# Issue order of the feed-forward stages of a two-layer encoder trunk: chunks earlier, sums in steps, tables in pieces, splits one output late

## The chip, the core and the metric

The kernel runs on one core of one Trainium2 chip. The metric is device time in microseconds (us) of one execution, the median of several runs. The core's engines work in parallel, each through its own instructions in a fixed order, and wait for each other by semaphores: TensorE (PE in the profile, with its weight loads as PEld) multiplies matrices, VectorE (DVE), ScalarE (ACT) and GpSimd (POOL) work elementwise, SyncE (SP) issues transfers. A result of PE lies in a bank of the accumulator memory until another engine has read it.

## The reference

A trunk of two layers on one sequence of 512 tokens of width 1024, all in float32. A layer is a half-step SwiGLU feed-forward stage, a mixer (latent attention, a bidirectional mLSTM and a Fourier part beside each other), a second feed-forward stage and a gated embedding:

```python
def swiglu(x, w_gate, w_up, w_down):
    return (jax.nn.silu(x @ w_gate) * (x @ w_up)) @ w_down
...
h = x
for i in range(DEPTH):                                    # DEPTH = 2
    h = h + 0.5 * swiglu(rmsnorm(h, ffn1_norm[i]), ffn1_w_gate[i], ffn1_w_up[i], ffn1_w_down[i])
    u = rmsnorm(h, mix_norm[i]) @ w_in[i]
    ...
    h = h + y @ w_out[i]
    h = h + 0.5 * swiglu(rmsnorm(h, ffn2_norm[i]), ffn2_w_gate[i], ffn2_w_up[i], ffn2_w_down[i])
    e = rmsnorm(p[i] @ ple_w_proj[i], ple_post_norm[i])
    gate = jax.nn.sigmoid(rmsnorm(h, ple_gate_norm[i]) @ ple_w_gate[i])
    h = h + gate * e
return rmsnorm(h, final_norm)
```

The inner width of a feed-forward stage is 2816, which is 22 features of 128. The attention turns parts of its queries and keys by rotary tables, cosine and sine of position times frequency.

## The kernel before, in words

**Precision by halves.** Every operand of a product is split into a high half, rounded to the matmul's type by a cast on ACT (line 134, or 353 and 415 where the split is written out), and a low half, the rest, by a subtraction on DVE (line 131, `lo_of`). A product is three matmuls: high by high, high by low, low by high (lines 161 to 163). So every weight costs an ACT cast and a DVE subtraction before PE can use it: a chunk is 128 x 1024 numbers (512 KB) that come by one transfer on SP's queue into `wraw` (two buffers) and are split into `whi` and `wlo` (three each).

**A feed-forward stage** (`ffn`, line 305) runs four times, with the mixer (`mix`) or the embedding gate (`ple`) behind it. Activations lie transposed, feature by token, in 8 rows of blocks `h[:, m]`. The first `PLAIN` = 4 features are computed plainly: a block of 24 matmuls for gate and one for up, then `gated` (DVE, ACT's silu, DVE, split). The other 18 features go by Strassen's scheme in Winograd's form with 7 products instead of 8: `p1` to `p7`, each 12 matmuls of 256 columns (line 451). On the weight side it takes the four sums S1 to S4 of quarters of the chunks: some are made by an adding transfer on POOL's queue (`acc`, line 427), two by DVE (`sums`, lines 436 and 438), and all are split by `parts` (lines 415 and 131). On the activation side it takes four sums T1 to T4, the same for all 18 features, which `combined` makes once per stage (lines 375 to 381: two scaled copies on ACT, two subtractions on POOL, two steps on DVE, a split), for four pairs of rows.

**One unit** u is a period of seven slots, in the order p6(u), p1(u+1), p7(u), p5(u+1), p4(u), p2(u+1), p3(u). p1, p6, p7 and p4 of one feature add up in one accumulator bank, and between them the bank is copied as it stands: `g1` behind p1 (line 478), `g2` behind p6 (516), `c22` behind p7 (526, and 527 on DVE). The next product into that bank waits for the copy. The rest of a unit is elementwise: lines 505 and 506 (DVE, POOL) behind p2, 536 and a split behind p4, 547 and 548 behind p3, the silus at 550 (at 594 for the first unit) and at 461, and 462 on POOL.

**Down parts.** After each group of units (`GROUPS`), a down part multiplies the group's features into all eight outputs, one block of three matmuls per feature and output; `flush` (lines 559 and 560) adds an output to `h`. In the last down part of a stage, `flush` also calls the next stage's `chunk` for the row: the high half `xh` on ACT (287), the low half `xl` on DVE (289), and a square on ACT with its addition on DVE (192, 193) for the next norm. The square root of that norm is taken by a chain of DVE steps (`wide`, lines 218 to 229) in the plain part of the next feed-forward stage, or by `tok` in the other stages.

**What sets the order.** The stage is a list written out by hand. `item(us, run, tasks)` gives a PE step a price by which a clock advances (5.6 for a plain block, 1.434 for a product, 0.7 per feature of a down output) and its preparing tasks with a lead each. All tasks are sorted by the clock of their item minus their lead, and a task is issued ahead of the first item whose clock has come to that. `tc.manual_schedule()` keeps this order on every engine. In the mixer that holds for PE alone, and elsewhere the scheduler chooses. Leads before: a chunk's transfer 12 and its split 7; transfers of quarters 17 or 24; sums and `parts` 7.

Of the kernel before, what the change touches and what calls it, by code (L numbers as in the profile page):

```python
# [10 lines left out]
F32 = mybir.dt.float32  # L11
# [20 lines left out]
LEAD = 5  # L32
H = T // 2
PLAIN = 4
GROUPS = (5, 5, 4, 4, 4)
NA = max(GROUPS) + 1
QD = 6
NB = HALF + 2
# [55 lines left out]
def trunk(ctx: ExitStack, tc, xT, pT, pos, W, gains, cst, dftc, out):  # L94
# [85 lines left out]
    class Norm:  # L180


        def __init__(self, n):
            self.n, self.acc = n, None

        def add(self, x):
            if self.acc is None:
                self.acc = sp.tile([P, T], F32, tag="sqacc", name="sqacc")
                S.activation(self.acc, x, AF.Square)
            else:  # L190
                sq = sp.tile([P, T], F32, tag="sq", name="sq", bufs=1)
                S.activation(sq, x, AF.Square)
                V.tensor_tensor(self.acc, self.acc, sq, op=ALU.add)

        def tok(self, by=None):

# [45 lines left out]
    sinT = cp.tile([P, T], F32, name="sinT")  # L242

    def rope_tables():
        def tile(tag, dt=F32, bufs=None):
            return sp.tile([P, T], dt, tag=tag, name="rope", bufs=bufs)

        pi = tile("sq", I32, 1)
        nc.scalar.dma_start(pi, pos)
        r = tile("rbc", bufs=3)  # L250
        V.tensor_copy(r, pi)
        V.tensor_scalar(r, r, cs[:, C_INV:C_INV + 1], None, op0=ALU.mult)
        k = tile("rbc", bufs=3)
        V.tensor_scalar(k, r, 1.0 / TWO_PI, None, op0=ALU.mult)
        big = 1.5 * 2.0 ** 23
        V.tensor_scalar(k, k, big, None, op0=ALU.add)
        V.tensor_scalar(k, k, -big, None, op0=ALU.add)
        k1 = tile("sqacc")
        big1 = 1.5 * 2.0 ** 34
        V.tensor_scalar(k1, k, big1, None, op0=ALU.add)  # L260
        V.tensor_scalar(k1, k1, -big1, None, op0=ALU.add)
        k0 = tile("sqacc")
        V.tensor_tensor(k0, k, k1, op=ALU.subtract)
        for m, cc in ((k1, _c1), (k0, _c1), (k1, _c2), (k0, _c2), (k, _c3)):
            V.scalar_tensor_tensor(r, m, -cc, r, op0=ALU.mult, op1=ALU.add)
        V.tensor_scalar(r, r, math.pi, -math.pi, op0=ALU.min, op1=ALU.max)
        sn = tile("sq", bufs=1)
        S.activation(sn, r, AF.Sin)
        S.activation(r, r, AF.Sin, scale=0.5)
        V.tensor_scalar(sinT, sn, cs[:, C_SGN:C_SGN + 1], None, op0=ALU.mult)  # L270
        V.tensor_tensor(r, r, r, op=ALU.mult)
        V.tensor_scalar(cosT, r, -2.0, 1.0, op0=ALU.mult, op1=ALU.add)


    h = hp.tile([P, NK, T], F32, name="h")

    class Stage:
# [5 lines left out]
            self.hi, self.lo = [None] * NK, [None] * NK  # L283

        def chunk(self, m, norm=True):
            xh = xp.tile([P, T], F32R, tag="xh", name="xh", bufs=NK)
            S.activation(xh, h[:, m], AF.Copy, scale=self.g(m))  # L287
            xl = xp.tile([P, T], F32R, tag="xl", name="xl", bufs=NK)
            V.scalar_tensor_tensor(xl, h[:, m], self.g(m), xh.bitcast(F32), op0=ALU.mult, op1=ALU.subtract)  # L289
            self.hi[m], self.lo[m] = xh, xl  # L290
            if norm:
                self.norm.add(h[:, m])

        def tok(self):
            self.rt = self.norm.tok()
# [9 lines left out]
    def ffn(l, cgu, cd, st, nxt, first=False):  # L305
# [5 lines left out]
        with tc.tile_pool(name="ap", bufs=1) as ap, tc.manual_schedule():  # L311
# [23 lines left out]
                return acts[f]  # L335


            def chunk_tasks(w, c, halves=False):

                if (l, c) in ahead:  # L340
                    w["hl"] = ahead.pop((l, c))
                    return []

                def dma():
                    w["raw"] = wp.tile([P, CHUNK], F32, tag="wraw", name="wraw", bufs=2)
                    nc.sync.dma_start(w["raw"], W[l, c])

                def prep():
                    hi = wp.tile([P, CHUNK], F32R, tag="whi", name="whi")
                    lo = wp.tile([P, CHUNK], F32R, tag="wlo", name="wlo")  # L350
                    for i in range(1 + halves):
                        b = slice(i * CHUNK // (1 + halves), (i + 1) * CHUNK // (1 + halves))
                        S.copy(hi[:, b], w["raw"][:, b])  # L353
                    lo_of(lo, w["raw"], hi)
                    w["hl"] = hi, lo

                return [(12.0, dma), (7.0, prep)]


            todo = []  # L360
            ready = 3 if first else 0
            Th, Tl = [], []

            def gated(f, pg, pu):
                t = qa()
# [5 lines left out]
            def combined(i):  # L371

                xg = tile("pw", 6, [2, T])
                for j in range(2):
                    S.activation(xg[:, j], h[:, i + 4 * j], AF.Copy, scale=st.g(i + 4 * j))
                t = tile("pw", 6, [4, H])
                (b11, b12), (b21, b22) = ((xg[:, j, 0:H], xg[:, j, H:T]) for j in range(2))
                G.tensor_tensor(t[:, 0], b11, b12, op=ALU.subtract)
                G.tensor_tensor(t[:, 1], b22, b12, op=ALU.subtract)
                V.scalar_tensor_tensor(t[:, 2], t[:, 0], -1.0, b22, op0=ALU.mult, op1=ALU.subtract)  # L380
                V.scalar_tensor_tensor(t[:, 3], t[:, 2], -1.0, b21, op0=ALU.mult, op1=ALU.subtract)
                hi, lo = tile("th", 4, [4, H], F32R), tile("tl", 4, [4, H], F32R)
                split(hi, lo, t)
                Th.append(hi)
                Tl.append(lo)

            def plain(f, i, w):
                def run():
                    if i == 0:
                        todo.append((f, bank("ps"), bank("pm")))  # L390
                    blocks(todo[-1][1 + i], *w["hl"], st)
                    n = 2 * f + i
                    if n == ready:
                        st.rb = st.norm.wide(qd)
                    if n > ready + 1 and i:
                        for x in todo:
                            gated(*x)
                        todo.clear()
                    if n > 2 * PLAIN - 5:
                        combined(n - 2 * PLAIN + 4)  # L400

                return run

# [65 lines left out]
            def p1(u, after=None):  # L469
                U[u] = {"gate": {}}  # L470

                def run():
                    d = U[u]
                    d["B"] = bank("ps")[:, 0:H]
                    hi, lo = d["gate"]["hl"]
                    product(u, "B", hi[:, 0:T], lo[:, 0:T], "B11", True)
                    d["g1"] = small("g1")
                    S.copy(d["g1"], d["B"])
                    if after is not None:
                        finish(after)  # L480

                return run, chunk_tasks(U[u]["gate"], cgu + 2 * u, True)

            def p5(u, after=None):
                def run():
# [53 lines left out]

                return run, load(u, "A22", 1) + [(7.0, lambda: parts(u, "A22"))]  # L540

            def p3(u, nxt_u):
                def run():
                    d = U[u]
                    p = d["w", "S4"]
                    product(u, "E", p[:, 0], p[:, 1], "B22", False)
                    V.tensor_tensor(d["g2"], d["g2"], d["E"], op=ALU.add)
                    G.tensor_tensor(d["g2"], d["g2"], st.rb[:, h2], op=ALU.mult)  # L548
                    if nxt_u is not None:
                        S.activation(U[nxt_u]["g1"], U[nxt_u]["g1"], AF.Silu)  # L550

                return run, [(7.0, lambda: parts(u, "S4"))]

# [3 lines left out]
            def flush(m, last):  # L557
# [1 line left out]
                V.tensor_tensor(y, pys.pop(m), st.rb, op=ALU.mult)  # L559
                V.scalar_tensor_tensor(h[:, m], y, 0.5, h[:, m], op0=ALU.mult, op1=ALU.add)  # L560
                if last:
                    nxt.chunk(m)

            def down(f0, nf, pieces, last):

                ws = {}
                for m, a, b in pieces:
                    tasks, new = [], []
                    for j in range((m * nf + a) // 8, (m * nf + b - 1) // 8 + 1):
                        if j not in ws:  # L570
                            ws[j] = {}
                            tasks += chunk_tasks(ws[j], cd + f0 + j)

                    def run(m=m, a=a, b=b):
                        if a == 0:
# [15 lines left out]
            put(SL, p1(PLAIN))  # L591
            put(SL, p5(PLAIN))
            put(SL, p2(PLAIN))
            item(0.0, lambda: S.activation(U[PLAIN]["g1"], U[PLAIN]["g1"], AF.Silu))
            g, f0 = 0, 0
            for u in range(PLAIN, NF - 1):
                prev = u - 1 if u > PLAIN else None
# [3 lines left out]
                put(SL, p5(u + 1, prev))  # L601
                put(SL, p4(u))
                put(SL, p2(u + 1))
                put(SL, p3(u, u + 1))
                if u == f0 + GROUPS[g]:
                    for x in down(f0, GROUPS[g], [(m, 0, GROUPS[g]) for m in range(NK)], False):
                        item(*x)
                    if first and g == 0:
                        item(0.0, late_constants)
                        item(0.0, rope_tables)  # L610
                    f0 += GROUPS[g]
                    g += 1
            u, n = NF - 1, GROUPS[g]
            order = [(0, 0, 2), (1, 0, 2), (2, 0, 3), (3, 0, 3), (0, 2, 4), (1, 2, 4), (2, 3, 4), (3, 3, 4)]
            ds = list(down(f0, n, order + [(m, 0, n) for m in range(4, NK)], True))
            put(SL, p6(u))
            item(*ds[0])
            item(0.0, lambda: finish(u - 1))
            put(SL, p7(u))
            item(*ds[1])  # L620
            item(0.0, lambda: finish2(u - 1))
            put(SL, p4(u))
            put(SL, p3(u, None))
            item(0.0, lambda: (finish(u), finish2(u)))
            for x in ds[2:]:
                item(*x)
# [881 lines left out]
```

## Time and profile before

| | |
|---|---|
| median of 3 runs | 2188.37 us (2185.84 to 2188.86) |
| the profiled execution | 2190.03 us, its span 2188.3 us |
| PE | busy 2035.9 us, 93% |
| DVE | busy 1565.4 us, 72% |
| ACT | busy 1015.5 us, 46% |
| POOL | busy 361.9 us, 17% |
| granted TensorE clock, mean | 0.966 |
| transfers | 244.23 MB, 240.06 MB of it read from memory, 111 GB/s over the span |

A row of a wait names the engine and line that waits, what released it, the total, how often, and the longest. A row of a timeline has the start, the duration, engine, line and operation, then output and inputs with their shapes, and in brackets the idle time before it and its releaser. A granted clock of 1.00 is full speed. The four feed-forward stages lie at about 6 to 409, 656 to 1027, 1108 to 1475 and 1725 to 2097 us.

### The profile page before, as it was taken

The page shows a single profiled execution, that of the slowest core. Times are in us where ns is not written, and L with a number is a line of the kernel's source. Part 1 is how long each engine was busy: PE and PEld are TensorE (multiplying, and loading weights), DVE is VectorE, ACT ScalarE, POOL GpSimd, SP SyncE. Part 2 cuts the span into 40 slices and gives each one's busy share as a digit, 9 for nine tenths or more (in the row PEclk, how much of TensorE's full clock was granted, in tenths as well). Part 3 has the DMA queues.
Part 4 walks back from the last instruction along what each step waited for, and adds up shares of the span by engine and source line. Part 5 has one row for each costly group of instructions (what it writes and reads, how often), then busy time and mean ns, then how long its engine had stood idle before and what let it go on. Part 6 is the DMA issues. An engine that isn't in the chain of part 4 may idle for free.

```text
span 2188.3 us, 31811 instructions
## 1 busy us (share of the span) xinstructions
PE 2035.9 (93%) x12216; PEld 1791.8 (82%) x12216; DVE 1565.4 (72%) x2607; ACT 1015.5 (46%) x1938; POOL 361.9 (17%) x415
## 2 busy tenths in 40 slices
PE   7789999899999899999998999998999989999987
PEld 5679999788777798987777989987877779899867
DVE  5677777677856677777766777776786666777777
ACT  4424444456633443444544434444575343444453
POOL 0213222000001232221002222310000022222200
PEclk9899999999999999999899999998999999999989
DMA  3345454221123445553224645522210235545421
GB/s 131 96 127 160 126 157 140 73 84 55 55 68 101 130 131 159 149 147 99 68 92 120 160 136 148 161 86 82 74 57 26 95 101 159 154 132 140 139 96 49
DMA packets 96664, 244.23 MB, mean 112 GB/s; under 512 B 10592, under 2 KB 14064, under 8 KB 96512
## 3 DMA queue, kind: packets, MB, share of 16 engines
q1 hardware_dynamic: 73488, 200.98, 27.3%
q0 software_dynamic: 20784, 37.84, 10.6%
q10 hardware_dynamic: 2240, 3.38, 0.5%
q8 instruction: 96, 1.57, 0.3%
q14 instruction: 56, 0.46, 0.1%
HBM read 240.06 MB, written 2.10 MB: 111 GB/s over the span
## 4 chain that ended last, share of the span: by engine, by line
PE 62%; DVE 17%; ACT 10%; issue 6%; POOL 3%; DMA 1%; ACTq 0%; DVEq 0%; POOLq 0%; SPq 0%
PE ps L451 12%; PE ps L163 8%; PE ps L162 8%; PE ps L161 8%; PE pm L161 7%; PE pm L163 7%; PE pm L162 7%; DVE wlo L131 4%; ACT pw L415 3%; ACT whi L353 2%; DVE pw L131 2%; PE pm L451 2%; DVE qa L436 2%; POOL g L548 1%; DVE g L505 1%
## 5 line engine op out<-in xcount | busy, mean ns | idle before, releaser
L451 PE MATMUL ps<-th,pw 128*128 128x256 f32 x2304 | 450.9, 288 | 48.2 <-ACT g L516 25.4
L451 PEld LDWEIGHTS ps<-th,pw 128*128 128x128 f32 x2304 | 374.9, 194 | 59.4 <-ACT g L516 33.6
L131 DVE TENSOR_TENSOR wlo<-wraw,whi 128x1024 fp32r<-128x1024 f32 (+3 forms) x275 | 324.5, 1181 | 79.2 <-ACT whi L134 38.4
L451 PE MATMUL ps<-tl,pw 128*128 128x256 f32 x1152 | 329.4, 286 | 0.0
L353 ACT CAST whi<-wraw 128x512 fp32r<-128x512 f32 (+1 forms) x261 | 203.4, 810 | 213.4 <-DMA wraw<-in_W 109.3
L451 PEld LDWEIGHTS ps<-tl,pw 128*128 128x128 f32 x1152 | 224.1, 195 | 0.9
L131 DVE TENSOR_TENSOR pw<-qa,pw 128x512 fp32r<-128x512 f32 x144 | 111.8, 776 | 86.8 <-ACT pw L415 85.0
L131 DVE TENSOR_TENSOR pw<-qd,pw 128x512 fp32r<-128x512 f32 x216 | 148.1, 687 | 10.9 <-ACT pw L415 5.9
L427 POOL DMA_DIRECT2D qd<-in_W x144 | 125.6, 912 | 176.6 <-DMA qd<-in_W 175.6
L161 PE MATMUL pm<-ah,whi 128*128 128x512 f32 x384 | 152.2, 396 | 0.0
L163 PE MATMUL pm<-ah,wlo 128*128 128x512 f32 x384 | 151.6, 395 | 0.0
L162 PE MATMUL pm<-al,whi 128*128 128x512 f32 x384 | 151.2, 394 | 0.0
L506 POOL TENSOR_TENSOR g<-g,rbc 128x256 f32<-128x256 f32 x72 | 72.5, 1007 | 387.4 <-DVE g L505 387.4
L134 ACT CAST whi<-wraw 128x1024 fp32r<-128x1024 f32 (+6 forms) x86 | 80.8, 943 | 116.9 <-PE ps L162 51.4
L161 PE MATMUL ps<-xh,whi 128*128 128x512 f32 x288 | 119.8, 416 | 15.7 <-ACT xh L287 12.5
L163 PE MATMUL ps<-xh,wlo 128*128 128x512 f32 x288 | 118.2, 410 | 10.8 <-DVE wlo L131 10.8
L161 PE MATMUL ps<-ah,whi 128*128 128x512 f32 x320 | 126.6, 396 | 0.0
L163 PE MATMUL ps<-ah,wlo 128*128 128x512 f32 x320 | 126.1, 394 | 0.0
L162 PE MATMUL ps<-al,whi 128*128 128x512 f32 x320 | 126.0, 394 | 0.0
L415 ACT CAST pw<-qd 128x512 fp32r<-128x512 f32 x216 | 124.0, 613 | 0.0
L162 PE MATMUL ps<-xl,whi 128*128 128x512 f32 x288 | 118.0, 410 | 1.2 <-DVE xl L289 1.1
L134 ACT CAST ah<-g 128x256 fp32r<-128x256 f32 x144 | 58.4, 406 | 124.8 <-DVE g L536 116.6
(390 smaller groups left out, 5214.0 us busy)
## 6 DMA issues: line engine op xcount, KB each, us to landing
wraw<-in_W SPq DMA_DIRECT2D x245, 512.0 KB, 3.6
qd<-in_W SPq DMA_DIRECT2D x216, 256.0 KB, 4.2
qd<-in_W POOLq DMA_DIRECT2D x144, 256.0 KB, 5.0
gr<-in_W SPq DMA_DIRECT2D x8, 512.0 KB, 3.9
wraw<-in_W SPq DMA_DIRECT2D x8, 320.0 KB, 2.8
wraw<-in_dftc SPq DMA_DIRECT2D x4, 516.0 KB, 3.4
h<-in_xT ACTq DMA_DIRECT2D x8, 256.0 KB, 4.2
wraw<-in_W SPq DMA_DIRECT2D x4, 408.0 KB, 3.0
```

What stands on the lines that cost most here:

```text
L131: V.tensor_tensor(lo, x, hi.bitcast(F32), op=ALU.subtract)
L134: S.copy(hi, x)
L161: mm(o, wh, xh, start=first, stop=False)
L162: mm(o, wh, xl, start=False, stop=False)
L163: mm(o, wl, xh, start=False, stop=last)
L353: S.copy(hi[:, b], w["raw"][:, b])
L415: S.copy(p[:, 0], U[u][src])
L427: nc.gpsimd.dma_start(U[u][name], up[:, T:2 * T] if add == "A22" else gate[:, 0:T], accum_op=ALU.add)
L436: V.tensor_tensor(d["S2"], raw[:, 0:T], d["S1"], op=ALU.add)
L451: mm(U[u][o], x[:, b], y, start=first and i + j == 0, stop=i == 3 and j == 2, skip_group_check=not first)
L505: V.tensor_tensor(d["g1"], d["g1"], d["A"], op=ALU.add)
L506: G.tensor_tensor(d["g1"], d["g1"], st.rb[:, h1], op=ALU.mult)
```

## The change

- Leads: a plain chunk's transfer 18 and split 12; a gate chunk's 15 and 9; a down chunk's 14 and 8.
- `combined` becomes a generator in two steps, the first (ACT and POOL) behind one plain block, the second (DVE and the split) behind the next, from the block at which the norm is made on (the fourth in the trunk's first stage, else the second).
- The rotary tables, which only the first feed-forward stage makes, are issued in three pieces behind the outputs 0, 4 and 6 of the first down part, not in one piece behind it.
- The silu of `g1` moves from behind p3 (and, for the first unit, from ahead of p6) to behind the copy of `g1` in the next unit's p1.
- In the last down part, the low half and the addition of the square of an output are issued behind the next output's elementwise steps; the high half and the square stay.
- Groups of (5, 4, 4, 4, 5) features, and a new order of the pieces of the last down part.

```diff
-GROUPS = (5, 5, 4, 4, 4)
+GROUPS = (5, 4, 4, 4, 5)
...
-        def add(self, x):
+        def square(self, x):
...
                 sq = sp.tile([P, T], F32, tag="sq", name="sq", bufs=1)
                 S.activation(sq, x, AF.Square)
+                self.sqs.append(sq)
+
+        def sum(self):
+            sq = self.sqs.pop(0)
+            if sq is not None:
                 V.tensor_tensor(self.acc, self.acc, sq, op=ALU.add)
...
         V.tensor_scalar(r, r, math.pi, -math.pi, op0=ALU.min, op1=ALU.max)
+        yield
         sn = tile("sq", bufs=1)
         S.activation(sn, r, AF.Sin)
         S.activation(r, r, AF.Sin, scale=0.5)
+        yield
...
+        def high(self, m, norm=True):
             xh = xp.tile([P, T], F32R, tag="xh", name="xh", bufs=NK)
             S.activation(xh, h[:, m], AF.Copy, scale=self.g(m))
+            self.hi[m] = xh
+            if norm:
+                self.norm.square(h[:, m])
+
+        def low(self, m, norm=True):
             xl = xp.tile([P, T], F32R, tag="xl", name="xl", bufs=NK)
+            V.scalar_tensor_tensor(xl, h[:, m], self.g(m), self.hi[m].bitcast(F32), op0=ALU.mult, op1=ALU.subtract)
...
+                self.norm.sum()
...
-            def chunk_tasks(w, c, halves=False):
+            def chunk_tasks(w, c, halves=False, lead=12.0):
...
-                return [(12.0, dma), (7.0, prep)]
+                return [(lead + 6.0, dma), (lead, prep)]
...
                 G.tensor_tensor(t[:, 1], b22, b12, op=ALU.subtract)
+                yield
                 V.scalar_tensor_tensor(t[:, 2], t[:, 0], -1.0, b22, op0=ALU.mult, op1=ALU.subtract)
...
                     if n == ready:
                         st.rb = st.norm.wide(qd)
+                    for x in making:
+                        next(x)
+                    making.clear()
+                    i0 = n - (3 if first else 1)
+                    if 0 <= i0 < 4:
+                        making.append(combined(i0))
+                        next(making[0])
                     if n > ready + 1 and i:
                         for x in todo:
                             gated(*x)
                         todo.clear()
-                    if n > 2 * PLAIN - 5:
-                        combined(n - 2 * PLAIN + 4)
...
                     S.copy(d["g1"], d["B"])
+                    if u > PLAIN:
+                        S.activation(U[u - 1]["g1"], U[u - 1]["g1"], AF.Silu)
                     if after is not None:
                         finish(after)
 
-                return run, chunk_tasks(U[u]["gate"], cgu + 2 * u, True)
+                return run, chunk_tasks(U[u]["gate"], cgu + 2 * u, True, 9.0)
...
                     G.tensor_tensor(d["g2"], d["g2"], st.rb[:, h2], op=ALU.mult)
-                    if nxt_u is not None:
-                        S.activation(U[nxt_u]["g1"], U[nxt_u]["g1"], AF.Silu)
...
                 if last:
-                    nxt.chunk(m)
+                    nxt.high(m)
+                    if m:
+                        nxt.low(m - 1)
+                    if m == NK - 1:
+                        nxt.low(m)
...
-                            tasks += chunk_tasks(ws[j], cd + f0 + j)
+                            tasks += chunk_tasks(ws[j], cd + f0 + j, lead=8.0)
...
-            item(0.0, lambda: S.activation(U[PLAIN]["g1"], U[PLAIN]["g1"], AF.Silu))
...
                 if u == f0 + GROUPS[g]:
-                    for x in down(f0, GROUPS[g], [(m, 0, GROUPS[g]) for m in range(NK)], False):
+                    rope = rope_tables() if first and g == 0 else None
+                    for m, x in enumerate(down(f0, GROUPS[g], [(m, 0, GROUPS[g]) for m in range(NK)], False)):
                         item(*x)
-                    if first and g == 0:
-                        item(0.0, late_constants)
-                        item(0.0, rope_tables)
+                        if rope and m in (0, 4, 6):
+                            if m == 0:
+                                item(0.0, late_constants)
+                            item(0.0, lambda rope=rope: next(rope))
...
-            order = [(0, 0, 2), (1, 0, 2), (2, 0, 3), (3, 0, 3), (0, 2, 4), (1, 2, 4), (2, 3, 4), (3, 3, 4)]
+            order = [(0, 0, 2), (1, 0, 2), (0, 2, n - 1), (1, 2, n - 1), (2, 0, n - 1),
+                     (0, n - 1, n), (1, n - 1, n), (2, n - 1, n), (3, 0, n)]
...
-            item(0.0, lambda: finish(u - 1))
+            item(0.0, lambda: (S.activation(U[u]["g1"], U[u]["g1"], AF.Silu), finish(u - 1)))
```

More of the change, by code (lines that the diff above doesn't have):

```diff
@@ L183, in __init__ @@
         def __init__(self, n):
-            self.n, self.acc = n, None
-        def add(self, x):
+            self.n, self.acc, self.sqs = n, None, []
+        def square(self, x):
             if self.acc is None:
@@ L189, in add @@
                 S.activation(self.acc, x, AF.Square)
+                self.sqs.append(None)
             else:
@@ L192, in add @@
                 S.activation(sq, x, AF.Square)
+                self.sqs.append(sq)
+        def sum(self):
+            sq = self.sqs.pop(0)
+            if sq is not None:
                 V.tensor_tensor(self.acc, self.acc, sq, op=ALU.add)
+        def add(self, x):
+            self.square(x)
+            self.sum()
         def tok(self, by=None):
@@ L285, in chunk @@
         def chunk(self, m, norm=True):
+            self.high(m, norm)
+            self.low(m, norm)
+        def high(self, m, norm=True):
             xh = xp.tile([P, T], F32R, tag="xh", name="xh", bufs=NK)
             S.activation(xh, h[:, m], AF.Copy, scale=self.g(m))
+            self.hi[m] = xh
+            if norm:
+                self.norm.square(h[:, m])
+        def low(self, m, norm=True):
             xl = xp.tile([P, T], F32R, tag="xl", name="xl", bufs=NK)
-            V.scalar_tensor_tensor(xl, h[:, m], self.g(m), xh.bitcast(F32), op0=ALU.mult, op1=ALU.subtract)
-            self.hi[m], self.lo[m] = xh, xl
+            V.scalar_tensor_tensor(xl, h[:, m], self.g(m), self.hi[m].bitcast(F32), op0=ALU.mult, op1=ALU.subtract)
+            self.lo[m] = xl
             if norm:
-                self.norm.add(h[:, m])
+                self.norm.sum()
         def tok(self):
@@ L355, in prep @@
                     w["hl"] = hi, lo
-                return [(12.0, dma), (7.0, prep)]
+                return [(lead + 6.0, dma), (lead, prep)]
             todo = []
             ready = 3 if first else 0
-            Th, Tl = [], []
+            Th, Tl, making = [], [], []
             def gated(f, pg, pu):
@@ L379, in combined @@
                 G.tensor_tensor(t[:, 1], b22, b12, op=ALU.subtract)
+                yield
                 V.scalar_tensor_tensor(t[:, 2], t[:, 0], -1.0, b22, op0=ALU.mult, op1=ALU.subtract)
@@ L385, in combined @@
                 Tl.append(lo)
+                yield
             def plain(f, i, w):
@@ L540, in p4, with p3 @@
                 return run, load(u, "A22", 1) + [(7.0, lambda: parts(u, "A22"))]
-            def p3(u, nxt_u):
+            def p3(u):
                 def run():
@@ L603, in ffn @@
                 put(SL, p2(u + 1))
-                put(SL, p3(u, u + 1))
+                put(SL, p3(u))
                 if u == f0 + GROUPS[g]:
-                    for x in down(f0, GROUPS[g], [(m, 0, GROUPS[g]) for m in range(NK)], False):
+                    rope = rope_tables() if first and g == 0 else None
+                    for m, x in enumerate(down(f0, GROUPS[g], [(m, 0, GROUPS[g]) for m in range(NK)], False)):
                         item(*x)
-                    if first and g == 0:
-                        item(0.0, late_constants)
-                        item(0.0, rope_tables)
+                        if rope and m in (0, 4, 6):
+                            if m == 0:
+                                item(0.0, late_constants)
+                            item(0.0, lambda rope=rope: next(rope))
                     f0 += GROUPS[g]
@@ L622, in ffn @@
             put(SL, p4(u))
-            put(SL, p3(u, None))
+            put(SL, p3(u))
             item(0.0, lambda: (finish(u), finish2(u)))
```

## The prediction

> **What bounds the kernel now.** I read the page's busy times and its chain first, then the engine waits of the whole span, then a table of stages.
>
> ```profile
> span 2188.3 us, 31811 instructions
> PE 2035.9 (93%) x12216; PEld 1791.8 (82%) x12216; DVE 1565.4 (72%) x2607; ACT 1015.5 (46%) x1938; POOL 361.9 (17%) x415
> PE 62%; DVE 17%; ACT 10%; issue 6%; POOL 3%; DMA 1%; ACTq 0%; DVEq 0%; POOLq 0%; SPq 0%
> ```
>
> PE is busy for 93%, but the chain that ends last is PE for only 62%: for the rest the end hangs on DVE and ACT. The change touches no matmul, so all it can do is shorten or lengthen PE's waits and the half-clock stretches behind them. The stages (columns: window, its length, busy time with instructions of PE, PEld, DVE, ACT and POOL, granted clock, DMA share, GB/s):
>
> ```profile
> 656.00:743.40 87.40, 76.13 (x401) 64.97 (x400) 56.45 (x78) 38.45 (x62) 14.96 (x17) 0.92 0.34 97
> 743.40:771.30 27.90, 27.90 (x123) 22.57 (x122) 16.75 (x23) 6.67 (x10) 4.92 (x6) 1.00 0.57 152
> 771.30:823.50 52.20, 50.98 (x422) 50.37 (x421) 41.64 (x69) 28.58 (x65) 17.41 (x19) 1.00 0.54 144
> 851.40:892.90 41.50, 40.70 (x338) 40.29 (x337) 33.30 (x55) 21.65 (x50) 13.27 (x15) 1.00 0.49 137
> 1027.00:1064.00 37.00, 27.44 (x109) 21.53 (x108) 26.16 (x47) 21.89 (x34) 0.00 (x0) 0.82 0.21 72
> ```
>
> They are: the entry of the second feed-forward stage (call the four F1 to F4) up to its first down part, that down part, its second and third group of units, and the last down going over into the embedding gate. Down parts and groups run at full clock and nearly dense; entries and exits do not. A block is priced at 5.6 us and a slot at 1.434 us by the kernel's planner, and the windows bear the second out: 28 slots are 40.15 of 41.50 us.
>
> **The change part by part.**
>
> *A, entries.* Eight plain blocks and 17 slots are 44.8 + 24.4 = 69.2 us, and the entry of F2 takes 87.4: 18.2 are lost. PE's waits in it, 640 to 712 us and then 708 to 745 us, and DVE's timeline:
>
> ```profile
> PE ps L163 <- DVE wlo L131: 3.4, 1, 3.4
> PE ps L451 <- ACT pw L415: 4.6, 1, 4.6
> PE ps L451 <- ACT g L516: 1.2, 1, 1.2
> 662.45 0.69 DVE L221 TENSOR_SCALAR qd<-pm 128x512 f32<-128x512 f32 x1 [1.75 <-PE pm L219]
> 670.53 2.35 DVE L131 TENSOR_TENSOR wlo<-wraw,whi 128x1024 fp32r<-128x1024 f32 x2
> ```
>
> The 3.4 us: the low half of the third chunk stands behind the norm's chain of elementwise steps (662.45 to 670.53, 8.1 us) on DVE. With chunk work 12 instead of 7 us ahead (two blocks of 5.6) it is issued before that chain, and the wait goes. The 4.6 us: product p5 (L451) needs the sums of activations, and the fourth `combined` stands behind the last plain block, with two gated outputs. Spread over the blocks, each in two halves, it is ready, and POOL's two subtractions no longer hold DVE. The 1.2 us: the copy at L516 stands behind the first silu (L594), which waits for POOL; that silu now stands behind two copies. Behind the long wait lies a slow stretch:
>
> ```profile
> 716.30:720.00 3.70, 3.13 (x13) 0.50 0.87 158
> 720.00:721.80 1.80, 1.80 (x13) 0.73 0.83 255
> 792.80:794.80 2.00, 1.60 (x14) 1.00 0.82 303
> ```
>
> A slot of 1.43 us takes 3.64 at clock 0.50 and the next 1.87: 2.6 us more, while the stretch at 792.8, behind a wait of 0.4, stays at 1.00. [...]
>
> Not all 18.2 come back. DVE is then what the plain stage waits for: the norm's 8.1 us, eight low halves of 1.18 and four pairs of elementwise steps in 45 us. I expect 1.1 us at the first gate chunk, 2 to 3 at p5 (low half of S1), 0.6 at p6, 1.2 at p4, and 1 to 2 of start, in all 7. F2 gains 11. F4's entry (87.1 us against 69.2) gains 11 as well, F3's (83.7, so 14.5 lost) 9; in F1, where the input rows have yet to land, I take 5:
>
> ```profile
> 1108.00:1191.70 83.70, 72.43 (x377) 61.66 (x378) 55.17 (x77) 37.11 (x60) 14.96 (x17) 0.90 0.34 101
> 1725.00:1812.10 87.10, 74.57 (x401) 63.67 (x400) 56.37 (x78) 38.46 (x62) 14.93 (x17) 0.94 0.33 97
> ```
>
> A is **-36**; if DVE's residues are double, -15; if none is left, -45.
>
> *B, rotary tables.* The PE wait of 139 to 160 us, and the DVE and ACT steps under it:
>
> ```profile
> PE ps L451 <- ACT g L516: 10.6, 1, 10.6
> 143.62 0.42 DVE L251 CAST rope<-rope 128x512 f32<-128x512 int32 x1
> 151.60 0.63 ACT L268 ACTIVATE rope<-rope 128x512 f32<-128x512 f32 x1 [20.38 <-DVE rope L266]
> ```
>
> The tables are issued behind the whole down part: 8.0 us of DVE, while the sine (L268) blocks ACT and L516 behind it, and PE waits 10.6. In three pieces inside the down's eight outputs (27.9 us in the stage table, with DVE busy for 16.75) they are covered; a piece can still put off a low half by 1 to 2 us. With the 2 us of slow slots behind the wait, B is **-10** (-8 to -12). Without that cover it is zero.
>
> *C, the loop of units.* Here I expect a loss. A unit is 7 slots, 10.04 us. In steady state DVE, ACT and POOL need more, as the timelines of one unit show (DVE, then ACT):
>
> ```profile
> 175.36 0.42 DVE L547 TENSOR_TENSOR g<-g,ps 128x256 f32<-128x256 f32 x1
> 177.97 0.82 DVE L131 TENSOR_TENSOR pw<-qa,pw 128x512 fp32r<-128x512 f32 x1 [1.59 <-ACT pw L415]
> 180.10 1.23 DVE L131 TENSOR_TENSOR wlo<-wraw,whi 128x1024 fp32r<-128x1024 f32 x1
> 181.25 0.42 DVE L536 SCALAR_TENSOR_TENSOR g<-ps,g 128x256 f32<-128x256 f32 x1
> 186.08 0.41 DVE L547 TENSOR_TENSOR g<-g,ps 128x256 f32<-128x256 f32 x1
> ```
>
> ```profile
> 177.01 0.42 ACT L461 ACTIVATE g<-g 128x256 f32<-128x256 f32 x1 [1.06 <-POOL g L548]
> 177.84 0.36 ACT L526 COPY c<-ps 128x256 f32<-128x256 f32 x1
> 178.93 1.14 ACT L353 CAST whi<-wraw 128x512 fp32r<-128x512 f32 x2
> 184.91 0.42 ACT L550 ACTIVATE g<-g 128x256 f32<-128x256 f32 x1 [1.77 <-POOL g L506]
> ```
>
> Around the cycle: L547 at 175.36, which L461 waits for by way of POOL (1.65), the cast of S4 (1.97), its low half (2.61), ..., L547 again at 10.72 (186.08). That is 0.68 us a unit more than PE's 10.04. PE feels it where the slack from the down before is used up, at L516 behind the silu L550, 0.57 us from the third unit of a group on:
>
> ```profile
> PE ps L451 <- ACT g L516: 1.2, 3, 0.4
> ```
>
> (in the second group of F2.) Its five units lose 2.0 us (52.20 less 35 slots), the third group 1.35, a whole stage 5.0. The change moves that silu behind the two copies, so this wait goes. But the gate chunk, 9 instead of 7 us ahead, now puts its two casts (1.14) and its low half (1.16) before L526 and L527. Recounted from the rows: S4 cast 1.97, casts 2.48 to 3.62, L526 at 3.52 to 3.9, low half of the gate chunk 3.64, L527 4.79, low half of S2 5.13, L536 6.08, and 4.83 from there as before: 10.91, or 0.87 a unit over PE. And p4, which writes the bank that L526 reads, starts 5.74 into the unit, so only 1.8 us of slack stands where 2.8 stood: waits of about 0.2, 1.0, 0.9, 0.8 in a group of four, 2.9 instead of 1.35. Three such groups and one with 1.6 make 10.2 a stage instead of 5.0. C is **+21**; from the far ends, -20 if the new order hides all of today's waits, +30 if the whole 0.87 shows in every unit with a slow first slot. I take +21, as every step of the recount has a row. Groups of (5, 4, 4, 4, 5) move one unit only. Two more edits I cost at nothing: the raw chunks' DMA, issued 3 us sooner on SP, finds its two buffers free one unit earlier, since the sums that read them are long done; and the sum of squares, now behind the next output, is read by the norm alone.
>
> *D, exits.* DVE and PE around the last down of F1, then PE's waits at that of F2:
>
> ```profile
> 410.58 0.69 DVE L559 TENSOR_TENSOR qa<-ps,rbc 128x512 f32<-128x512 f32 x1
> 412.78 0.75 DVE L289 SCALAR_TENSOR_TENSOR xl<-h,gv,xh 128x512 fp32r<-128x512 f32 x1 [0.79 <-ACT xh L287]
> 413.45 0.68 DVE L193 TENSOR_TENSOR sqacc<-sqacc,sq 128x512 f32<-128x512 f32 x1
> 414.05 0.68 DVE L559 TENSOR_TENSOR qa<-pm,rbc 128x512 f32<-128x512 f32 x1
> PE ps L669 <- DVE qa L559: 8.7, 2, 6.3
> PE ps L161 <- DVE qa L559: 5.1, 1, 5.1
> PE ps L161 <- ACT e L1253: 3.0, 1, 3.0
> ```
>
> An output costs DVE 3.47 us (410.58 to 414.05), 0.79 of it waiting for its own high half, against PE's 2.8 for four rows, so DVE ends late and the next stage waits for a bank. Splitting one output late removes the 0.79: 2.7 us, below PE's 2.8, or 3.5 for the five rows of the new last group. Only the last outputs' tail stays. Of the mixer's 8.7 I take 7 back, twice; of the gate's 8.1 and of the 4.9 us that clock 0.82 costs its 27.4 busy us, 11, twice: D is **-36** (-25 to -45).
>
> Sum: -36 - 10 + 21 - 36 = -61, made against the profiled execution's 2190.0 (span 2188.3 and 1.7 around it): 2129. The median of the runs is 1.7 below that execution, so **2128** on its scale.
>
> **Rivals.** *The loop follows PE after all*: copies wait less than I count, because ACT (28.6 busy of 52.2) has room; then C is -20 and the time 2128 - 41 = 2087. For it: 1.0 us of PE's slack already covers most of 0.87; against: the order on each engine is fixed. *DVE takes the place*: entries and exits give half (-18, -18) since DVE's work is only moved, 2164. For it: DVE is busy 56 of 87 in the entry, with chains that wait on ACT. *Slower*: the gate casts, now ahead of L526, wait for their raw chunk in every unit, between DMA issue (15 us ahead) and cast (9). All behind them in the cycle shifts by as much, in 68 of 72 units; from 0.9 us (61 / 68) on it decides, and at 1.5 us the time is 2128 + 102 = 2230. For it: the whole span has such waits of up to 13.8 us at L353; against: none of size lies in the loops, and 6 us stand for a landing of 3.6:
>
> ```profile
> ACT whi L353 <- DMA wraw<-in_W: 109.3, 19, 13.8
> wraw<-in_W SPq DMA_DIRECT2D x245, 512.0 KB, 3.6
> ```
>
> *It doesn't do what it says*: the sums of activations are still late, since the plain run is bound by DVE, and the exits wait for ACT instead; with C as forecast nothing is left, 2186.
>
> **How the numbers follow.** Forecast 0.52 (own range 2108 to 2148), loop on PE 0.18, half back 0.18, no effect 0.05, slower 0.07. From 2090 to 2168 holds the forecast, the half case and part of the loop case. A measurement of this kernel tells 0.2% (4.4 us) from nothing: faster 0.89, same 0.03, slower 0.08.
>
> **What would show it.** A: no PE wait over 3 us at p5, and no slot at clock 0.50 there. B: no wait at L516 in 139 to 160. C: PE's waits in the loops at p4, released by the copy of c22, from the first or second unit of a group on, and none at L516; a unit of some 10.9 us. D: DVE's outputs 2.7 to 2.8 us apart with no wait for ACT, and the mixer's first wait for a bank under 2 us. I am wrong if groups of four take 40.2 us (loop on PE), or if entries still take 80 us and more.

## The result, and the profile after

The changed kernel takes 2130.31 us (median of 4 runs, 2127.25 to 2131.46) against 2187.11 us before (4 runs): a ratio of 0.9738, with a 95% interval of 0.9721 to 0.9755. The forecast was 2128. The page's span, busy times and chain after:

```profile
span 2129.7 us, 31784 instructions
PE 2020.9 (95%) x12216; PEld 1775.7 (83%) x12216; DVE 1554.3 (73%) x2607; ACT 1019.9 (48%) x1938; POOL 376.3 (18%) x415
PE 56%; DVE 21%; ACT 13%; issue 7%; POOL 2%; DMA 1%; ACTq 0%; DVEq 0%; POOLq 0%; SPq 0%
```

The same matmuls stand in 58.6 us less of span, yet the chain that ends last is less of PE (56% after 62%) and more of DVE and ACT. That fits a change that took long waits away and left a cycle of DVE and ACT as the bound of the groups. PE's waits over the whole span (engine, line and releaser: us in total, times, longest), first at the copy of `g2` before, then the four largest after:

```profile
PE ps L451 <- ACT g L516: 25.4, 32, 10.6
```

```profile
PE ps L481 <- ACT c L558: 22.7, 42, 0.6
PE ps L161 <- ACT xh L305: 14.3, 5, 6.2
PE ps L481 <- ACT whi L376: 12.2, 3, 10.3
PE ps L481 <- ACT pw L445: 9.0, 4, 3.8
```

Products are line 481 now, and L558 is the copy of c22. The wait for it is new, 42 times, and heads the list, as forecast; the wait at the copy of `g2` is gone. In stages (columns as before: window, length, busy time of each engine, granted clock, DMA share, GB/s), the entries of F2 and F4, the third group of F1 and the exit of F2:

```profile
636.10:714.00 77.90, 72.96 (x400) 62.37 (x399) 56.07 (x79) 38.68 (x63) 15.60 (x17) 0.98 0.38 110
1680.40:1758.30 77.90, 72.95 (x400) 62.38 (x399) 56.09 (x79) 38.48 (x62) 15.60 (x17) 0.98 0.39 110
200.90:243.70 42.80, 41.12 (x337) 40.31 (x336) 34.05 (x56) 23.08 (x53) 13.38 (x15) 1.00 0.46 128
1002.20:1029.00 26.80, 24.48 (x106) 18.73 (x105) 20.91 (x38) 19.52 (x30) 0.00 (x0) 0.94 0.30 98
```

The entry of F2 is down from 87.4 to 77.9, the exit into the gate from 37.0 to 26.8, but a group of four units is up from 41.5 to 42.8. I cut both spans at the same matmuls (first of a first down part, last of a last down part, first of the next stage; a mixer's start ends at its first matmul of line 161, some 20 us in). The differences add up to the 58.6:

| part | forecast | measured |
|---|---|---|
| A, entries F1, F2, F3, F4 | -5, -11, -9, -11 | -3.9, -9.5, -8.2, -9.2 (-30.7) |
| B, rotary tables (F1 alone) | -10 | -8.0 with F1's loop; about -12 without it |
| C, loops F2, F3, F4 | +5.2 each | +4.4, +4.2, +4.4 |
| D, mixers and gates | -7, -11, -7, -11 | -6.6, -9.6, -6.9, -9.3 (-32.3) |
| bodies of the two mixers | 0 | -0.6 |

### The profile page after: what moved, and what is told of

Same layout as the page of the kernel before. It is cut to its first block, busy times and chain, and to the rows that moved or that the text cites. A ratio compares the mean times of both kernels' runs of the same rounds, so it can differ in the third digit from the quotient of the medians.

```text
span 2129.7 us, 31784 instructions
## 1 busy us (share of the span) xinstructions
PE 2020.9 (95%) x12216; PEld 1775.7 (83%) x12216; DVE 1554.3 (73%) x2607; ACT 1019.9 (48%) x1938; POOL 376.3 (18%) x415
## 4 chain that ended last, share of the span: by engine, by line
PE 56%; DVE 21%; ACT 13%; issue 7%; POOL 2%; DMA 1%; ACTq 0%; DVEq 0%; POOLq 0%; SPq 0%
PE ps L481 9%; PE ps L162 7%; PE ps L161 7%; PE ps L163 7%; PE pm L161 6%; PE pm L162 6%; PE pm L163 6%; DVE wlo L131 5%; ACT whi L376 4%; ACT pw L445 3%; DVE pw L131 3%; DVE qa L466 2%; POOL g L580 2%; PE pm L481 2%; ACT g L491 1%
## 5 line engine op out<-in xcount | busy, mean ns | idle before, releaser
L481 PE MATMUL ps<-th,pw 128*128 128x256 f32 x2304 | 458.0, 287 | 33.1 <-ACT c L558 22.7
L131 DVE TENSOR_TENSOR pw<-qa,pw 128x512 fp32r<-128x512 f32 x144 | 107.5, 746 | 92.7 <-ACT pw L445 92.7
L538 POOL TENSOR_TENSOR g<-g,rbc 128x256 f32<-128x256 f32 x72 | 84.6, 1175 | 379.6 <-DVE g L537 379.6
L548 ACT COPY g<-ps 128x256 f32<-128x256 f32 x72 | 26.9, 373 | 232.6 <-PE ps L481 232.6
L445 ACT CAST pw<-qd 128x512 fp32r<-128x512 f32 x216 | 119.7, 616 | 0.0
```

Source lines behind the costliest of these rows:

```text
L131: V.tensor_tensor(lo, x, hi.bitcast(F32), op=ALU.subtract)
L445: S.copy(p[:, 0], U[u][src])
L481: mm(U[u][o], x[:, b], y, start=first and i + j == 0, stop=i == 3 and j == 2, skip_group_check=not first)
L538: G.tensor_tensor(d["g1"], d["g1"], st.rb[:, h1], op=ALU.mult)
```

## Experiments

Kernels timed together share a chip and their runs of before, so I compare each kernel by its ratio to before. Where a run is set against after, its ratio is divided by 0.9738 and multiplied by 2130; both intervals are some 0.16% wide to each side, so such a difference is known to about 5 us.

### The gate chunk's lead alone, 7 again

```diff
-return run, chunk_tasks(U[u]["gate"], cgu + 2 * u, True, 9.0)
+return run, chunk_tasks(U[u]["gate"], cgu + 2 * u, True, 9.0 if u < PLAIN + 2 else 7.0)
```

> After with one edit: from the third Strassen unit on, the gate chunk's split has lead 7 as before, not 9 (the first two keep 9). Theory (the gate chunk's casts stand ahead of the copy of c22 and lengthen the cycle of DVE, ACT and POOL): the cycle goes from 10.9 back to 10.7 us a unit, the waits at p4 start only at the third unit of a group, each stage gains about 4.3 us, so 2113 (2109 to 2117). Rival (the wait at p4 comes from the moved silu or from DVE's amount of work, not from the gate chunk): within 4 us of 2130.

2125.19 us, ratio 0.9722 (0.9706 to 0.9738): 3.5 us below after, no difference that can be told. By its number the rival holds and my theory misses. ACT's timeline at the last unit of a group, in this run, and PE's waits in the third group of F1 show why:

```profile
172.97 0.60 ACT L445 CAST pw<-qa 128x512 fp32r<-128x512 f32 x1
173.48 1.04 ACT L376 CAST whi<-wraw 128x1024 fp32r<-128x1024 f32 x1
174.43 0.36 ACT L558 COPY c<-ps 128x256 f32<-128x256 f32 x1
```

```profile
PE ps L481 <- ACT c L558: 1.7, 2, 1.4
```

The cast ahead of the copy of c22 is now that of a *down* chunk (1024 columns in one piece), which the change also issues a step sooner, at lead 8. In the last unit of a group it costs 1.4 us and takes back most of what the gate chunk gave. Not all: the units before it take 10.71 us in this trace, not 10.88, as the theory had it, and a group of four is 0.5 us shorter than in after. So the number that fits the rival doesn't show the rival's cause. I had left the down chunk's lead out of part C.

### Both chunk leads at 7

```diff
-tasks += chunk_tasks(ws[j], cd + f0 + j, lead=8.0)
+tasks += chunk_tasks(ws[j], cd + f0 + j, lead=7.0)
```

(with the edit above.)

> After with lead 7 for the gate chunks from the third unit on and for the down chunks, as before. Theory (in the run with the gate chunk alone moved back, the down chunk's cast, 8 us ahead, stood before the copy of c22 in the last unit of each group and cost 1.5 us there; with both behind the copy, 0.6 us a unit from the second unit on is left): 2110 to 2118. Rival (the cycle of 10.7 us against PE's 10.04 is the whole loss, and where its wait stands makes no difference): 2122 to 2127.

2109.97 us, ratio 0.9648 (0.9633 to 0.9663), 20 us below after and clear of both intervals. PE's waits in the whole span, and the third group of F1:

```profile
PE ps L481 <- ACT c L558: 11.4, 29, 0.4
```

```profile
199.20:240.70 41.50, 40.72 (x337) 40.28 (x336) 33.67 (x56) 23.07 (x52) 13.07 (x15) 1.00 0.46 124
```

The theory holds, at the low end of its range, and the rival falls. The wait at the copy of c22 halves, and a group takes 41.5 us as it did before the change. So the loss that the change brings to the loop is that of the sooner leads: two casts of a chunk ahead of c22's copy, the gate's in all units but the last of a group, the down's in that one. The forecast's 21 us for C has its size here, measured by undoing the leads.

### The silu of g1 back at its old place

```diff
-if u > PLAIN:
-    S.activation(U[u - 1]["g1"], U[u - 1]["g1"], AF.Silu)
...
+if nxt_u is not None:
+    S.activation(U[nxt_u]["g1"], U[nxt_u]["g1"], AF.Silu)
```

> After with the silu of g1 back at its old place behind p3 (ahead of p6 for the first unit). Theory (p4's slack of 1.8 us runs out before p7's 2.8, so the silu's place no longer matters in the loop): no new waits at the copy of g2 in the groups, only the wait of about 1.2 us at the first p7 of each stage comes back, 2130 to 2136. Rival (the silu's move is worth the 0.57 us a unit that it cost before): 0.6 us in most of 72 units, 2150 to 2170.

2125.69 us, ratio 0.9722 (0.9707 to 0.9737), again no difference from after that can be told, 3.5 us lower rather than the few higher that I had. PE's waits over the whole span (L556 is the copy of c22 in this kernel):

```profile
PE ps L481 <- ACT c L556: 22.1, 40, 0.6
PE ps L481 <- ACT g L546: 1.4, 2, 0.8
```

The wait at the copy of `g2` (L546) comes back twice, 1.4 us in all, and not in most units, as the rival had it. The loop stops at p4 before p7's slack is used up: in this kernel the silu's move is worth nothing by itself.

### finish behind the copy of c22, alone and with the gate's lead

`finish` is the silu of `g2` on ACT and its product with c22 on POOL. It moves from behind the copy of `g1` in p1 to behind the copy of c22 in p7.

```diff
                     S.copy(d["g1"], d["B"])
...
-                    if after is not None:
-                        finish(after)
...
                     V.scalar_tensor_tensor(d["c22"], d["E"], -1.0, d["c22"], op0=ALU.mult, op1=ALU.subtract)
+                    if after is not None:
+                        finish(after)
```

> After with one edit: finish (silu of g2, its product on POOL) is issued behind the copy of c22 in p7, not behind the copy of g1 in p1. Theory (DVE idles 1.6 us a unit for the cast of S4, which stands on ACT behind that silu, which waits for POOL, which waits for DVE): the cycle falls from 10.9 to about 10.0 us, most waits at p4 go, 2095 to 2105. Rival (DVE's amount of work, 34 of 43 us in a group, and the place of the gate chunk set the cycle): under 10 us of gain, 2120 to 2130.

2092.37 us, ratio 0.9568 (0.9554 to 0.9582): 37 us below after, and 3 us below the range of my theory. DVE's timeline over one unit, from one L579 (the addition to `g2` behind p3) to the next, in after and in this run, and this run's third group of F1 in the stage columns:

```profile
148.53 0.42 DVE L579 TENSOR_TENSOR g<-g,ps 128x256 f32<-128x256 f32 x1
151.13 0.82 DVE L131 TENSOR_TENSOR pw<-qa,pw 128x512 fp32r<-128x512 f32 x1 [1.59 <-ACT pw L445]
159.41 0.42 DVE L579 TENSOR_TENSOR g<-g,ps 128x256 f32<-128x256 f32 x1
```

```profile
209.78 0.42 DVE L579 TENSOR_TENSOR g<-g,ps 128x256 f32<-128x256 f32 x1
211.33 0.69 DVE L131 TENSOR_TENSOR pw<-qa,pw 128x512 fp32r<-128x512 f32 x1 [0.52 <-ACT pw L445]
219.83 0.41 DVE L579 TENSOR_TENSOR g<-g,ps 128x256 f32<-128x256 f32 x1
```

```profile
197.00:237.10 40.10, 40.10 (x337) 40.10 (x336) 33.65 (x56) 23.13 (x52) 14.90 (x15) 1.00 0.51 137
```

After, a unit takes 10.88 us from L579 to L579, 1.59 of it DVE's wait for the cast of S4, which stands on ACT behind `finish`, which waits for POOL, which waits for that same L579. With `finish` behind the copy of c22 the wait is 0.52 and a unit takes 10.05, which is PE's own pace; PE is busy for all of the group. DVE's busy time there is the same as after (33.65 and 34.05), so the rival, DVE's amount of work, falls: it was the order.

The run with `finish` and the gate's lead together:

> The two edits together. Theory: the cycle falls below PE's 10.04 us, the groups run at PE's pace (40.2 us for four units), 10 us a stage less than after: 2090 (2086 to 2096). Rival (POOL's product, now later, holds the second split of the unit before on ACT, and takes the gain back): 2105 to 2120.

2094.93 us, ratio 0.9582 (0.9567 to 0.9597), as with `finish` alone, within what can be told. The lead has nothing left to give here: in the two traces a group of four, from its first product to its last, is even 0.4 us longer with it (40.7 against 40.3 us). The rival, a gain taken back by POOL's later product, falls.

### The same edit on the kernel before

> The kernel before with the edit of fin7 alone (finish behind the copy of c22 in p7). Theory (before too, DVE's idle 1.6 us behind POOL and ACT makes the cycle 10.7 us): the groups go at PE's pace, 16 to 20 us off, 2167 to 2172. Rival (before, the wait is that of the silu of g1 behind POOL's product, in each unit alike): 2183 to 2190.

2202.59 us, ratio 1.0071 (1.0055 to 1.0088): *slower* by 15 us, against both my numbers. PE's waits in the whole span, and ACT's timeline of one unit, in this run:

```profile
PE ps L451 <- ACT g L514: 35.3, 46, 10.6
```

```profile
184.67 0.42 ACT L550 ACTIVATE g<-g 128x256 f32<-128x256 f32 x1 [1.76 <-POOL g L504]
185.50 0.36 ACT L514 COPY g<-ps 128x256 f32<-128x256 f32 x1
187.65 0.37 ACT L524 COPY c<-ps 128x256 f32<-128x256 f32 x1 [0.99 <-PE ps L451]
195.48 0.42 ACT L550 ACTIVATE g<-g 128x256 f32<-128x256 f32 x1 [1.77 <-POOL g L504]
```

A unit takes 10.81 us here (10.72 before), though DVE no longer waits for S4. The copy of `g2` (L514) stands behind the silu (L550), which waits 1.76 us for POOL; p7 waits for that copy, the copy of c22 for p7, and now `finish` and all behind it for c22, on to the DVE step that POOL waits for. So I read two cycles longer than PE's 10.04, one through the silu ahead of `g2`'s copy, one through `finish` ahead of S4's cast. Cutting the first alone gives nothing (after, against the run with the silu put back), cutting the second alone costs 15 us (this run, against before), and both together (the silu's move is in after) bring the groups to 40.1. These runs stand on two kernels with different leads. That the silu is what holds this run is read from its trace: both edits together, and nothing else, weren't run on before, nor `finish` moved in after with the silu put back.

### The exits: no lag, and the old groups

```diff
-nxt.high(m)
-if m:
-    nxt.low(m - 1)
-if m == NK - 1:
-    nxt.low(m)
+nxt.chunk(m)
```

> After with the low half and the square's addition of an output issued right behind its high half again (last down parts). Theory (DVE's 0.79 us of waiting per output made the exits late): most of the 32 us of the four exits comes back, 2148 to 2160. Rival (five rows, 3.5 us of PE, cover 3.47 us of DVE just as well, so the gain is that of the group's size and the pieces' order): within 6 us of after, 2128 to 2136.

2156.5 us, ratio 0.986 (0.9845 to 0.9874), 27 us above after. DVE's timeline in the last down part of F1, after and in this run:

```profile
382.67 0.68 DVE L589 TENSOR_TENSOR qa<-pm,rbc 128x512 f32<-128x512 f32 x1
385.26 0.69 DVE L589 TENSOR_TENSOR qa<-pm,rbc 128x512 f32<-128x512 f32 x1
```

```profile
385.32 0.69 DVE L589 TENSOR_TENSOR qa<-pm,rbc 128x512 f32<-128x512 f32 x1
387.52 0.75 DVE L312 SCALAR_TENSOR_TENSOR xl<-h,gv,xh 128x512 fp32r<-128x512 f32 x1 [0.79 <-ACT xh L305]
388.79 0.69 DVE L589 TENSOR_TENSOR qa<-pm,rbc 128x512 f32<-128x512 f32 x1
```

2.59 us an output with the lag, 3.47 without it, of which 0.79 is the wait that the forecast named. The rival, that five rows (3.5 us of PE) cover 3.47 us as well, misses the first outputs. Their pieces end close together, so four of them stand back to back on DVE; ACT casts the next down chunk only behind the fourth one's high half, and PE waits for that cast, which it doesn't in after:

```profile
392.46 0.50 PE L161 MATMUL ps<-ah,whi 128*128 128x512 f32 x1 [2.29 <-ACT whi L376]
```

> After with the groups (5, 5, 4, 4, 4) and the old order of the pieces of the last down part. Theory (the exits' gain is that of the lag: 2.72 us of DVE an output lie under 2.8 of PE with four rows too): 2 to 8 us more than after, 2130 to 2138. Rival (the five-row last part is what gives DVE its room): 2142 to 2152.

The groups and the pieces' order of before, in after: 2140.88 us, ratio 0.9789 (0.9774 to 0.9805), 11 us above after, between the two expectations and nearer to the rival's range, so neither is shown. PE's wait at the exits to the mixers, 2.2 us in two waits in after:

```profile
PE ps L704 <- DVE qa L589: 9.1, 2, 4.6
```

So the lag matters most for D, and the groups with their order of pieces matter too. How much is each one's own can't be told: 27 and 11 add up to more than the 32 that both gave, as they would if each works in part only with the other, but each of the two is known to about 5 us.

### The entries: sums late, plain chunks at lead 7

> After with the four activation sums made as before, behind the last four plain blocks and behind the gated outputs, each in one go. Theory (p5 waited 4 to 6 us for them, with slow slots behind): 5 to 7 us a stage come back, 2150 to 2158. Rival (the plain stage is bound by DVE's total work, wherever the sums stand): within 6 us of after.

2145.66 us, ratio 0.9809 (0.9793 to 0.9824): 15 us above after, about 4 a stage, under the 5 to 7 that I gave, but outside the rival's 6 in all (L480 is a product in this kernel). PE's wait at p5 in F2 in this run:

```profile
PE ps L480 <- ACT pw L444: 5.7, 1, 5.7
```

In after it is 1.7 (next section); the 5.7 less 1.7 are the 4.

> After with the plain chunks' split at lead 7 and their transfer at 13 (before: 7 and 12). Theory (the third chunk's low half again stands behind the norm's chain, 3.4 us of PE): the waits of 3 us come back in three or four stages, 2137 to 2144. Rival (PE then only waits less for DVE later, at the first gate chunk and at p5): within 4 us of after.

2136.97 us, ratio 0.9769 (0.9753 to 0.9786), 7 us above after, at the low end of the theory and outside the rival's 4. PE's waits in the entry of F2 in this run:

```profile
PE ps L163 <- DVE wlo L131: 3.4, 1, 3.4
```

The 3.4 us behind the norm's chain are back, as long as they were before the change. But p5 then waits 0.6 instead of 1.7, so a part of what the sooner chunk gains is paid again at p5, as the rival had it.

### The rotary tables behind the down part

> After with the rotary tables issued in one piece behind the first down part again. Theory: PE waits some 10 us again behind that down part, 2140 to 2142. Rival (the loop behind it, whose waits are DVE's, absorbs a part): 2132 to 2136.

2142.68 us, ratio 0.9794 (0.9779 to 0.9808), 12 us above after, as the theory had it; the rival falls. PE waits 10.6 us at the copy of `g2` again, as before the change:

```profile
PE ps L481 <- ACT g L548: 10.6, 1, 10.6
```

### A faster version

`finish` behind c22, and the gated outputs in step: the products by the norm and the silus of all, then the products by up and the casts of all, then the low halves:

```diff
-for x in todo:
-    gated(*x)
+gated(todo)
```

> The edit of fin7 (2092), and the gated outputs of a plain run issued in step: all products by the norm and all silus, then all products by up and all casts, then all low halves, in place of one output after the other. Theory (DVE waits 0.7 us twice an output for ACT, and the first gate chunk's cast stands behind that chain, 10.4 us of PE in the first stage): 4 to 5 us less in the first stage, 1 us in each other, 2083 to 2088. Rival (the wait goes over to p5): 2090 to 2093.

2076.5 us, ratio 0.9499 (0.9481 to 0.9518): the fastest of all, 5% below before, 15 us below `finish` alone (0.9568) and beyond what I expected. ACT's timeline in the entry of F1, and PE's wait for the first gate chunk there (products are L484 in this kernel):

```profile
59.15 1.68 ACT L391 ACTIVATE qa<-qa 128x512 f32<-128x512 f32 x3
60.73 1.64 ACT L394 CAST ah<-qa 128x512 fp32r<-128x512 f32 x3
```

```profile
PE ps L484 <- ACT whi L376: 5.2, 1, 5.2
```

Three silus and three casts stand back to back, and the wait of 10.3 us (the longest in the list of after) is 5.2. From the spans, the entry of F1 gains 5.7 us over `finish` alone and the other three about 3 each, not 1.

## Why the prediction was right, point by point

The four parts went the way that was forecast, each somewhat off in size. That the sum is only some 2 us off is in part luck: A and D fell short by 5 and 4 us, B and C were better than forecast by 2 and 4.

**A** came out at -30.7 of -36. The entries kept 8.7 us over their 69.2, not the 7 taken: of the waits named, two show in the entry of F2 after, at p5 (1.7 us for 2 to 3) and at the first gate chunk (1.0 for its cast and 1.3 for its low half, for 1.1), and those at p6 and p4 don't,

```profile
PE ps L481 <- ACT pw L445: 1.7, 1, 1.7
PE ps L481 <- DVE wlo L131: 1.3, 1, 1.3
PE ps L481 <- ACT whi L376: 1.0, 1, 1.0
```

but what was left out stands behind these three, a stretch at half clock (here the columns are window, length, PE's busy time, granted clock, DMA share, GB/s):

```profile
683.50:686.80 3.30, 1.94 (x12) 1.00 0.92 258
686.80:690.20 3.40, 1.39 (x9) 1.00 0.43 75
690.30:693.60 3.30, 3.30 (x17) 0.50 0.90 192
```

Of the parts, the sums are worth 15 us and the plain chunks' lead 7; the rest, some 8, wasn't taken apart. The signs to look for were met only in part: in F2, F3 and F4 p5 waits less than 3 us, in F1 still 3.8, and slots at clock 0.50 were not gone. In F1 the change also brings a wait of its own, which the forecast had at 1.1 us for F2: the first gate chunk's cast stands on ACT behind the gated outputs, and PE waits 10.3 us for it, where before a plain block waited 6.1 for a chunk's cast and the gate chunk didn't wait. The clock behind it is 0.50 for all of the next 11.6 us:

```profile
PE pm L161 <- ACT whi L353: 6.1, 1, 6.1
```

```profile
74.40:86.00 11.60, 6.68 (x26) 0.50 0.60 97
```

Two workings of A don't hold. "If none is left, -45" doesn't follow from its terms, which give about -56 (18.2, 14.5 and 17.9 lost in F2 to F4, and F1's 5). And the row at 0.73 is the mean over a change of the clock, not a clock of its own; in other windows before shows

```profile
714.20:720.90 6.70, 4.04 (x17) 0.50 0.73 136
721.00:721.80 0.80, 0.80 (x9) 1.00 0.91 305
```

so the half clock already held under the wait and for 4.6 us behind it, not only the 3.7 of the prediction's row, and the 2.6 us lost there hold a further wait of 0.55 us.

**B** is -12 for the -10 forecast, on the edge of its range, by the direct run. The cover was there: DVE has 7.9 us of tables from 113.9 us on, under PE's down part.

```profile
113.94 0.42 DVE L262 CAST rope<-rope 128x512 f32<-128x512 int32 x1
121.92 0.63 ACT L280 ACTIVATE rope<-rope 128x512 f32<-128x512 f32 x1 [1.82 <-DVE rope L277]
```

The sine waits 1.82 us for DVE, not 20.38, since ACT reaches it late.

**C**, the forecast's one loss, is there: 10.88 us a unit for the 10.91 counted, a wait at the copy of c22 from the first units on, +4.2 to +4.4 a stage for +5.2. What the step missed was the second cast in the same place. The recount had the gate chunk's alone, and took the last unit of a group like the others; there the down chunk's cast does the work. That the number came out all the same is luck: the two casts happen to be of nearly one length (1.14 and 1.04 us).

**D** is -32 of -36, by the wait and the durations named; DVE's outputs stand 2.59 us apart for the 2.7 forecast. The mixers were right to half a us, the gates gave 1.4 to 1.7 less than 11. A wait that the forecast didn't have stands at the exits: PE waits for the sum of squares at both mixers and the last gate, before at that gate alone (before, then after):

```profile
PE pm L199 <- DVE sqacc L193: 3.4, 1, 3.4
```

```profile
PE pm L209 <- DVE sqacc L199: 6.0, 3, 2.3
```

The lag alone doesn't explain it, since the run without the lag has 2.2 us of it at the first mixer, after 2.3. That it stood hidden behind the longer wait for a bank is likely, but not shown.

**The rivals.** "The loop follows PE" did not come true of this change but of `finish` moved, with 2092 for the 2087 it was priced at: the price was right and the condition missed, since the order of ACT had to change once more. "Half back" and "doesn't do what it says" fall with A and D. The slower rival's mechanism, raw chunks landing late in every unit, doesn't show: in after no cast of a gate chunk on ACT waits for its transfer in the groups. At the end of a group a down chunk's cast does, by 0.6 to 1.9 us, and within a down part a gate or down chunk's, by up to 5.4 us.

## What to carry to other kernels

Where several engines hand work round in a circle, write the circle out with start times from one unit of the timeline and compare its length with the bounding engine's period; here a small excess (0.68 us a unit before, 0.84 after, 10.88 less 10.04) showed as a wait at a copy, that of `g2` before (25.4 us in all, 10.6 of it behind the rotary tables) and that of c22 after (22.7 us), and moving one of that copy's neighbours, the gate chunk's casts, left it at 24.0 us. Look for all circles: here two had nearly the same length by my reading, and cutting one was worth nothing in one kernel, cutting the other cost 15 us in another. A step that is issued sooner stands ahead of something else on its engine, as the casts of 1.14 and 1.04 us did here, so list what, for each kind of chunk that the edit touches.

## What was not expected of the hardware

In these traces the half clock stood behind short waits too. Before, in the entry of F2, the clock was 0.50 from 673.2 to 676.5 us, behind the single wait of 3.4 us, and under and behind that of 4.6 us; but also from 704.0 to 707.2, behind waits of 0.89 and 0.72 us, with PE busy for 1.39 of the 3.00 us from 701.0 on. After, no wait there is longer than 1.7 us, but by the three rows under A PE is busy for only 1.39 of the 3.40 us from 686.8 on, and then the clock is 0.50 for 3.3 us. Behind the stretch ahead of that, with 1.94 busy of 3.30 us, it stays at 1.00. The prediction took waits of 1 to 3 us to cost only themselves, and that doesn't hold here. By these rows it was not the length of a single wait alone that went with the half clock; which rule sets it was not shown.
